# A two-layer gated-attention block: its opening, its norm factors and its layout of values

## The chip, the cores and the metric

The kernel runs on one core of a Trainium2 chip. The time is the device time of one execution in microseconds (us); the median of three executions is given. A profile of one further execution shows what each engine did. PE is TensorE, ACT is ScalarE, DVE is VectorE, POOL is GpSimd, SP is SyncE.

## The reference, cut to what matters

Two layers act on x, 512 positions of 1024 features, in f32. In each layer a root-mean-square norm stands ahead of one wide projection `w_in`, which gives queries, keys and values of three attention branches and three gates; the branches' outputs are gated, summed and projected, and a second norm and an MLP follow.

```
h = _rms_norm(x, attn_norm[l])            # x * rsqrt(mean(x*x) + 1e-6) * g
proj = h @ w_in[l]                        # a_q a_k a_v | b_ql b_kvl b_kr | c_q c_k c_v | gate
aq, ak = rope(_rms_norm(a_q)), rope(_rms_norm(a_k))   # branch A: 3 groups of 4 heads of 64
o_a = _dilated_mixture(aq, ak, a_v)
...                                       # branch B: low-rank softmax attention, 8 heads
...                                       # branch C: stick-breaking attention, 8 heads of 64
merged = gates[0]*(o_a @ wbA) + gates[1]*(o_b @ wbB) + gates[2]*(o_c @ wbC)
x = x + merged @ w_out[l]
x = x + square(relu(_rms_norm(x, mlp_norm[l]) @ w_ff1[l])) @ w_ff2[l]
```

## The kernel before

x is kept transposed, as 8 tiles of 128 features by 512 positions. Every operand of a product is split into a high and a low half (fp32r), and a product is made of three: high by high, high by low, low by high (`mm3`, L298 to L302, and the same three in `denseA`, L427 to L429). So one 128x1024 chunk of weights is loaded by SP's queue into one of two raw buffers (`wload`, L270), its high half is cast on ACT and its low half subtracted on DVE (`wsplit`, L279), both with raised priority (`Early`), and 24 products with 512 columns each use it. Chunks come in the order of `ORDER` (L36); `qk0`, the queries and keys of branch A's first group, is the first block, in 4 chunks of 2 feature tiles each; `v0`, its values and 32 shared key columns (`kr`), is the second, in 3 chunks; `g00`, a gate, is the third.

A planner orders the instructions of each engine. It takes them by priority, which is the order of the program, raised by 80 places for what is issued through `Early`, as soon as its own costs say that they are ready; on the chip each engine then runs its list in that order.

**The norm.** `norm_tile` (L382) takes one feature tile: its high half with the gain on ACT and its low half on DVE, which are the operands of the products, and its square on ACT, added up over the tiles on DVE (`nacc`; the first is copied on POOL, L392). The products use x times the gain without the norm's factor, and the factor is put on when a result leaves PSUM. `norm_end` (L396) makes that factor in two shapes. `rcol` has one value for each position on the partitions, in natural order (columns 0 to 3) and in the order of residues modulo 4 (columns 4 to 7): 16 products of `hl` by two columns of ones (L405, L406), then `rsqrt`. `rrep` has it along the free axis, the same on all partitions: two products of a matrix of ones by `hl` (L412, L413) and `rsqrt` on 128x512. `rsqrt` (L314) is Ln and Exp on ACT and three operations on DVE. In each layer `norm_end(True)` stands in the program ahead of `layer(l)`, that is ahead of `qk0`.

**The opening.** SP's queue takes x's first tile, the gains, the first chunk, x's second tile, the second chunk, the other x tiles, three tables of constants and then the further chunks, each once a raw buffer is free. ACT's first instruction loads its function table. Before the first product stand the load and the cast of the whole first chunk.

**Blocks by position.** `denseB` (L441) computes `qk0` and `v0` with the positions on the PSUM partitions, in four PSUM tiles; chunks are the outer loop, so all four tiles finish during the last chunk, and each is then evacuated on ACT with `rcol` as scale (`raw_evac`). `qk0` uses two PSUM tiles of tag `d` and two of tag `s`; `v0` uses three `d` and one `o`; `g00` takes a `d`. There are 3 `d`, 2 `s`, 2 `t` and 1 `o`. After `qk0` its queries are normed and rotated by a chain on DVE and ACT (`head_norm`, L453), transposed on PE (`to_qT`, L495), then the same for the keys (`to_kbd`, L520), which are written into a tile `kT` whose other half is zero. `kbd_open` fills those halves with four copies on DVE for each layer (L507, L508).

**Values.** A value tile holds for each head 64 high and 64 low columns (`VS`). `vs_evac` (L722) writes them with the order swapped in every second head, and so by two instructions on ACT and two on DVE for each PSUM tile, one for the even and one for the odd heads; in `v0` the `kr` columns of the same PSUM tile are read after them. The attention's last product sums the high and low rows of its output in `finish_o`, whichever stands first.

Of the kernel before, what the change touches and what calls it, by code (L numbers as in the profile page):

```python
# [223 lines left out]
class Kern:  # L224
    BUFS = dict(
        raww=2, hl=3, a4=13, x2=9, gt=3, tmp=3, ot=1, sm=8, sm8=4, sm2=4, sm8b=2, u4=16,
        raw=2, qT=2, kT=2, SN=9, PT=2, VS=1, PR=2, st=6, mx=8, PP=2, sq=2,
# [100 lines left out]

    def setup(self, es):
# [5 lines left out]
        nc.scalar.add_instruction(  # L335
            mybir.InstLoadActFuncSet(name=nc.get_next_instruction_name(), act_func_set_id=ACT_SET, ins=[], outs=[])
        )
# [3 lines left out]
        self.bcol = k([96, L, 2], "bcol")  # L341
        for j in range(KT):
# [3 lines left out]
            if j == 0:  # L346
                nc.sync.dma_start(self.gain, self.ins["gain"])
            if j in self.wl0:
                self.wload(1 + self.wl0.index(j))
# [18 lines left out]
        self.ones = k([P, P], "ones")  # L368
        nc.vector.memset(self.ones, 1.0)
        self.onesr = k([P, P], "onesr", F32R)  # L370
        nc.vector.tensor_copy(self.onesr, self.ones)
        self.zero = k([P, 1], "zero")
        nc.gpsimd.memset(self.zero, 0.0)
# [7 lines left out]
    def norm_tile(self, j, x):  # L381
# [6 lines left out]
        sq = self.t(self.cp, "tmp", [P, S])  # L388
        nc.scalar.activation(sq, x, AF.Square)
        if self.nacc is None:  # L390
            self.nacc = self.t(self.cp, "x2", [P, S])
            nc.gpsimd.tensor_copy(self.nacc, sq)  # L392
        else:
            nc.vector.tensor_tensor(self.nacc, self.nacc, sq, ALU.add)

    def norm_end(self, cols):  # L396
# [4 lines left out]
        if cols:  # L401
            pc = self.ps("o")
            for t in range(NT):
                for c, sl in ((t, slice(t * P, t * P + P)), (4 + t, slice(t, None, 4))):
                    nc.tensor.matmul(pc[:, 2 * c : 2 * c + 2], hl[:, 0, sl], self.onesr[:, :2], start=True, stop=False)  # L405
                    nc.tensor.matmul(pc[:, 2 * c : 2 * c + 2], hl[:, 1, sl], self.onesr[:, :2], start=False, stop=True)  # L406
            a = self.small()[:, :8]
            nc.vector.tensor_scalar(a, pc[:, 0:16:2], 1.0 / D, EPS, ALU.mult, ALU.add)
            self.rcol = self.kp.tile([P, 8], F32, tag="rcol", name=self.nm("rcol"))
            self.rsqrt(self.rcol, a, self.kp, "sm8", [P, 8])  # L410
# [4 lines left out]
        nc.vector.tensor_scalar(a, ps, 1.0 / D, EPS, ALU.mult, ALU.add)  # L415
        self.rrep = self.kp.tile([P, S], F32, tag="rrep", name=self.nm("rrep"))
# [15 lines left out]
    def denseB(self, names, nk, n, evac, res=False, tags="dddo"):  # L432
# [3 lines left out]
        for name, m in zip(names, nk):  # L436
            w = self.wget(name)
# [62 lines left out]
    def kbd_open(self, n):  # L500
# [221 lines left out]
    def vs_evac(self, vs, h0, col, n=4):  # L722

        def f(t, ps):
            v = vs[:, t, h0 : h0 + n].rearrange("p (a b) c -> p a (b c)", b=2)
            src = ps[:, : 64 * n].rearrange("p (a b d) -> p a b d", b=2, d=64)
            for b in range(2):
                h = v[:, :, 192 * b : 192 * b + 64]
                lo = v[:, :, 64 + 64 * b : 128 + 64 * b]
                self.split(h, lo, src[:, :, b], col[:, t : t + 1], early=True)  # L730
        return f

    def layer(self, l):
# [262 lines left out]
        def block(name, n, evac, res=False, tags="dddo"):  # L996
            nk = [3, 3, 2] if name == "v0" else [2] * 4
            self.denseB([(l, name, i) for i in range(len(nk))], nk, n, evac, res, tags)

        def d_qk(i):  # L1000
            def f():
# [9 lines left out]
                block(f"qk{i}", 512, evac, i > 0, "dddo" if i else self.qktags)  # L1011
            return f

        def d_v0():
# [296 lines left out]

    ratio = 0.8
# [5 lines left out]
    qktags = "ddss"  # L1318
# [4 lines left out]
    def run(self, es):  # L1323
# [11 lines left out]
        for l in range(L):  # L1335
            self.norm_end(True)
# [26 lines left out]
```

## Time and profile before

| what | value |
| --- | --- |
| median of 3 runs (lowest, highest) | 1842.45 us (1841.03, 1843.02) |
| the profiled execution: its time, its span | 1844.2 us, 1842.4 us |
| busy share PE, PE's weight loads, DVE, ACT, POOL | 98%, 82%, 63%, 51%, 3% |
| mean granted clock of PE | 0.997 |
| DMA, mean over the span | 101 GB/s |

Times in the rows below are in us from the span's start unless marked ns. A timeline row is: start, duration, engine, line, operation, out<-in with shapes, number of instructions, and in brackets the engine's idle time before it and what ended that. A "q" behind an engine is its sequencer. Products overlap on PE, so the distance between two starts tells their price better than their duration. L219 is the helper through which `Early` issues.

### The profile page before, as it was taken

How to read it: one execution, taken by the hardware profiler on the slowest of the kernel's cores; microseconds unless marked ns; L12 is line 12 of the kernel's file. 1: busy time of each engine (PE TensorE's matmuls, PEld its weight loads, DVE VectorE, ACT ScalarE, POOL GpSimd, SP SyncE). 2: the span in 40 equal slices, each digit the busy share in tenths (PEclk: the TensorE clock that was granted, in tenths of full speed). 3: DMA queues.
4: the chain of work that ended last, by engine and by line, in shares of the span. 5: the costliest groups of instructions: out<-in, count | busy, mean ns of one | idle time of the engine just before them, and what ended most of it. 6: DMA issues, size and time to landing. Idle time of an engine off the chain costs nothing.

```text
span 1842.4 us, 23299 instructions
## 1 busy us (share of the span) xinstructions
PE 1811.3 (98%) x8672; PEld 1518.9 (82%) x8672; DVE 1165.8 (63%) x2131; ACT 937.4 (51%) x1763; POOL 50.7 (3%) x92
## 2 busy tenths in 40 slices
PE   8999999999999999999999999999999999999999
PEld 6899888777788888888888998887777888888887
DVE  6575789969875434444565657998788753434342
ACT  5644677867744323323445456777767442323231
POOL 3000001000000000000010000000000000000000
PEclk9999999999999999999999999999999999999999
DMA  4222241232363232333322221422233533333332
GB/s 163 86 87 94 62 142 58 86 103 92 109 194 98 92 103 92 103 92 103 126 92 77 89 89 58 138 69 95 94 98 117 187 92 99 96 96 99 96 99 92
DMA packets 64705, 186.90 MB, mean 101 GB/s; under 512 B 11472, under 2 KB 11984, under 8 KB 64592
## 3 DMA queue, kind: packets, MB, share of 16 engines
q1 hardware_dynamic: 57888, 178.93, 30.3%
q0 software_dynamic: 1952, 6.29, 0.9%
q8 instruction: 69, 1.13, 0.2%
q10 hardware_dynamic: 4752, 0.18, 0.2%
q14 instruction: 44, 0.36, 0.1%
HBM read 168.55 MB, written 16.78 MB: 101 GB/s over the span
## 4 chain that ended last, share of the span: by engine, by line
PE 85%; DVE 7%; ACT 6%; issue 1%; DMA 1%; ACTq 0%; SPq 0%; DVEq 0%
PE psd L429 20%; PE psd L428 20%; PE psd L427 20%; PE psd L300 3%; PE psd L302 3%; PE psd L301 3%; PE pst L695 2%; PE pss L300 1%; DVE SN L960 1%; PE pss L951 1%; PE pss L302 1%; PE pss L301 1%; PE pso L302 1%; PE pso L300 1%; PE pso L301 1%
## 5 line engine op out<-in xcount | busy, mean ns | idle before, releaser
L219 ACT CAST hl<-raww 128x1024 fp32r<-128x1024 f32 (+1 forms) x286 | 298.4, 1044 | 651.6 <-PE psd L429 483.5
L427 PE MATMUL psd<-a,hl 128*128 128x512 f32 x1232 | 485.8, 394 | 2.2 <-ACT kr L219 2.2
L429 PE MATMUL psd<-a,hl 128*128 128x512 f32 x1232 | 485.4, 394 | 0.0
L428 PE MATMUL psd<-a,hl 128*128 128x512 f32 x1232 | 484.9, 394 | 0.0
L219 DVE TENSOR_TENSOR hl<-raww,hl 128x1024 fp32r<-128x1024 f32 (+1 forms) x286 | 346.9, 1213 | 163.5 <-ACT hl L219 163.4
L427 PEld LDWEIGHTS psd<-a,hl 128*128 128x128 f32 x1232 | 232.0, 188 | 46.5 <-ACT kr L219 2.6
L428 PEld LDWEIGHTS psd<-a,hl 128*128 128x128 f32 x1232 | 232.0, 188 | 44.9 <-issue 0.3
L429 PEld LDWEIGHTS psd<-a,hl 128*128 128x128 f32 x1232 | 232.0, 188 | 44.4
L428 PE MATMUL psd<-u,hl 128*128 128x512 f32 (+1 forms) x648 | 250.4, 386 | 0.0
L429 PE MATMUL psd<-u,hl 128*128 128x512 f32 (+1 forms) x648 | 250.4, 386 | 0.0
L427 PE MATMUL psd<-u,hl 128*128 128x512 f32 (+1 forms) x648 | 250.4, 386 | 0.0
L1300 DVE TENSOR_TENSOR x<-x,psd 128x512 f32<-128x512 f32 x63 | 43.3, 687 | 184.6 <-PE psd L429 184.6
L429 PEld LDWEIGHTS psd<-u,hl 128*128 128x128 f32 x648 | 121.7, 188 | 24.7
L427 PEld LDWEIGHTS psd<-u,hl 128*128 128x128 f32 x648 | 121.7, 188 | 24.7
L428 PEld LDWEIGHTS psd<-u,hl 128*128 128x128 f32 x648 | 121.7, 188 | 24.6
L1281 DVE SCALAR_TENSOR_TENSOR tmp<-psd,rrep 128x512 f32<-128x512 f32 x64 | 44.3, 692 | 151.5 <-PE psd L429 151.4
L300 PE MATMUL psd<-hl,a 128*128 128x512 f32 (+3 forms) x328 | 122.9, 376 | 10.4 <-ACT hl L219 7.9
L302 PE MATMUL psd<-hl,a 128*128 128x512 f32 (+3 forms) x328 | 123.5, 377 | 0.0
L301 PE MATMUL psd<-hl,a 128*128 128x512 f32 (+3 forms) x328 | 123.2, 376 | 0.0
L219 ACT ACTIVATE gt<-gt 128x512 f32<-128x512 f32 x144 | 90.3, 630 | 28.9 <-DVE gt L219 23.3
L300 PEld LDWEIGHTS psd<-hl,a 128*128 128x128 f32 x328 | 80.0, 244 | 15.4 <-ACT hl L219 7.9
L301 PEld LDWEIGHTS psd<-hl,a 128*128 128x128 f32 x328 | 80.1, 244 | 4.4 <-DVE hl L219 0.8
(249 smaller groups left out, 2455.9 us busy)
## 6 DMA issues: line engine op xcount, KB each, us to landing
raww<-w SPq DMA_DIRECT2D x278, 512.0 KB, 3.6
gpark<-gt SPq DMA_DIRECT2D x48, 256.0 KB, 2.5
gt<-gpark SPq DMA_DIRECT2D x48, 256.0 KB, 3.6
x<-xT SPq DMA_DIRECT2D x8, 256.0 KB, 6.4
x<-xT POOLq DMA_DIRECT2D x8, 256.0 KB, 4.8
park<-x POOLq DMA_DIRECT2D x8, 256.0 KB, 2.3
x<-park POOLq DMA_DIRECT2D x8, 256.0 KB, 4.6
outT<-x SPq DMA_DIRECT2D x7, 256.0 KB, 2.0
```

The costliest lines, as they stand in the source:

```text
L219: return f(*a, **k)
L300: mm(ps, ah, bh, start=start, stop=False)
L301: mm(ps, ah, bl, start=False, stop=False)
L302: mm(ps, al, bh, start=False, stop=stop)
L427: self.nc.tensor.matmul(o, w[:, 0, c : c + P], t[:, 0], start=k == 0, stop=False)
L428: self.nc.tensor.matmul(o, w[:, 0, c : c + P], t[:, 1], start=False, stop=False)
L429: self.nc.tensor.matmul(o, w[:, 1, c : c + P], t[:, 0], start=False, stop=k == last)
L695: nc.tensor.transpose(ps[:, kt * P : kt * P + P], s[:, kt * P : kt * P + P], self.ident)
L951: nc.tensor.matmul(ps[:, :m], q[:, hh, sl], k[:, i, hh, :m], start=i == 0, stop=False)
L960: nc.vector.tensor_tensor_scan(e_[:, ::-1], self.ones[:, :1].to_broadcast([P, n]), c_[:, ::-1], 0.0, ALU.mult, ALU.add)
L1281: nc.vector.scalar_tensor_tensor(t, ps, 0.0, self.rrep, ALU.max, ALU.mult)
L1300: nc.vector.tensor_tensor(x, x, ps, ALU.add)
```

## The change: what it does

- The first chunk is loaded as two transfers of half its columns, which are one feature tile each, and split by two casts and two subtractions.
- x's first tile and the gains are issued by ACT's queue, and the function table is loaded after them.
- `warm`: the matrices of ones are made first, and PE issues 8 products of them, 128x128 in plain f32, into a PSUM tile that nothing reads.
- The first square is written straight into `nacc`; POOL's copy goes.
- `norm_end(True)` is called inside `qk0`, just ahead of its fourth chunk. The 16 narrow products go; `rcol` is read off the diagonal of the 128x128 blocks of the replicated sums, by 8 multiply-and-add reductions on DVE with the identity, and its `rsqrt` is made in two halves of 4 columns.
- `kbd_open`'s four copies go from DVE to POOL.
- Values have the high columns first in every head: one instruction on ACT and one on DVE for each PSUM tile. In `v0` the `kr` columns are read first.

```diff
@@ wload, wsplit
-            self.nc.sync.dma_start(t[:, :n], src)
+            for c in self.halves(self.nload, n):
+                self.nc.sync.dma_start(t[:, c], src[:, c])
...
+    def halves(self, i, n):
+        return [slice(0, n // 2), slice(n // 2, n)] if i == 0 else [slice(0, n)]
...
-            self.hs.copy(hl[:, 0, :n], raw[:, :n])
-            self.hv.tensor_tensor(hl[:, 1, :n], raw[:, :n], hl[:, 0, :n].bitcast(F32), ALU.subtract)
+            for c in self.halves(i, n):
+                self.hs.copy(hl[:, 0, c], raw[:, c])
+                self.hv.tensor_tensor(hl[:, 1, c], raw[:, c], hl[:, 0, c].bitcast(F32), ALU.subtract)
@@ setup
+        ps = self.ps("o")
+        for i in range(self.nwarm):            # 8
+            nc.tensor.matmul(ps[:, :P], self.ones, self.ones, start=True, stop=True)
...
-            nc.sync.dma_start(xt, self.ins["xT"][j])
+            if j == 0:
+                nc.scalar.dma_start(xt, self.ins["xT"][j])
+                nc.scalar.dma_start(self.gain, self.ins["gain"])
+                nc.scalar.add_instruction(... InstLoadActFuncSet ...)
+            else:
+                nc.sync.dma_start(xt, self.ins["xT"][j])
@@ norm_tile
-        sq = self.t(self.cp, "tmp", [P, S])
+        first = self.nacc is None
+        if first:
+            self.nacc = self.t(self.cp, "x2", [P, S])
+        sq = self.nacc if first else self.t(self.cp, "tmp", [P, S])
         nc.scalar.activation(sq, x, AF.Square)
-        if self.nacc is None:
-            self.nacc = self.t(self.cp, "x2", [P, S])
-            nc.gpsimd.tensor_copy(self.nacc, sq)
-        else:
+        if not first:
             nc.vector.tensor_tensor(self.nacc, self.nacc, sq, ALU.add)
@@ norm_end
-        if cols:
-            pc = self.ps("o")
-            for t in range(NT):
-                for c, sl in ((t, slice(t * P, t * P + P)), (4 + t, slice(t, None, 4))):
-                    nc.tensor.matmul(pc[:, 2 * c : 2 * c + 2], hl[:, 0, sl], self.onesr[:, :2], start=True, stop=False)
-                    nc.tensor.matmul(pc[:, 2 * c : 2 * c + 2], hl[:, 1, sl], self.onesr[:, :2], start=False, stop=True)
...
         nc.vector.tensor_scalar(a, ps, 1.0 / D, EPS, ALU.mult, ALU.add)
+        if cols:
+            self.rcol = self.kp.tile([P, 8], F32, tag="rcol", name=self.nm("rcol"))
+            c = self.small()
+            for i in range(2):
+                for t in range(NT):
+                    sl = slice(t, None, 4) if i else slice(t * P, t * P + P)
+                    nc.vector.tensor_tensor_reduce(
+                        out=self.t(self.kp, "dg", [P, P]), in0=a[:, sl], in1=self.ident, op0=ALU.mult, op1=ALU.add,
+                        scale=1.0, scalar=0.0, accum_out=c[:, 4 * i + t : 4 * i + t + 1],
+                    )
+                self.rsqrt(self.rcol[:, 4 * i : 4 * i + 4], c[:, 4 * i : 4 * i + 4], self.kp, "sm8", [P, 4])
@@ denseB(..., last=None)
+            if last is not None and name is names[-1]:
+                last()
             w = self.wget(name)
@@ kbd_open
-            nc.vector.tensor_copy(k[0:64, :, 1, :], z[0:64].to_broadcast([64, 2, S]))
-            nc.vector.tensor_copy(k[64:128, :, 0, :], z[64:128].to_broadcast([64, 2, S]))
+            nc.gpsimd.tensor_copy(k[0:64, :, 1, :], z[0:64].to_broadcast([64, 2, S]))
+            nc.gpsimd.tensor_copy(k[64:128, :, 0, :], z[64:128].to_broadcast([64, 2, S]))
@@ vs_evac
-            v = vs[:, t, h0 : h0 + n].rearrange("p (a b) c -> p a (b c)", b=2)
-            src = ps[:, : 64 * n].rearrange("p (a b d) -> p a b d", b=2, d=64)
-            for b in range(2):
-                h = v[:, :, 192 * b : 192 * b + 64]
-                lo = v[:, :, 64 + 64 * b : 128 + 64 * b]
-                self.split(h, lo, src[:, :, b], col[:, t : t + 1], early=True)
+            v = vs[:, t, h0 : h0 + n]
+            src = ps[:, : 64 * n].rearrange("p (h d) -> p h d", d=64)
+            self.split(v[:, :, 0:64], v[:, :, 64:128], src, col[:, t : t + 1], early=True)
@@ d_qk, d_v0, run
+                    block("qk0", 512, evac, False, "ddss", lambda: self.norm_end(True))
...
             def evac(t, ps):
+                self.hs.activation(kr[:, t], ps[:, 256:288], AF.Copy, scale=self.rcol[:, t : t + 1])
                 ev(t, ps)
-                self.hs.activation(kr[:, t], ps[:, 256:288], AF.Copy, scale=self.rcol[:, t : t + 1])
...
-            self.norm_end(True)
             self.layer(l)
```

## Rows read from the trace of the kernel before

**Rows 1.** The page's first part: busy us, share of span, instructions of each engine.
```profile
PE 1811.3 (98%) x8672; PEld 1518.9 (82%) x8672; DVE 1165.8 (63%) x2131; ACT 937.4 (51%) x1763; POOL 50.7 (3%) x92
```
**Rows 2.** Waits of PE, whole span: who, for whom, us in total, times, longest.
```profile
PE psd L300 <- ACT hl L219: 7.9, 1, 7.9
...
PE psd L427 <- ACT kr L219: 2.2, 2, 1.1
...
PE pst L520 <- DVE raw L475: 2.1, 4, 0.9
```
**Rows 3.** Stretches after sparse PE work: length, busy by engine, clock, DMA share, GB/s.
```profile
26.20:30.10 3.90, 3.90 (x12) 3.04 (x12) 2.31 (x6) 1.95 (x5) 0.15 (x1) 0.56 0.18 68
...
933.20:938.20 5.00, 5.00 (x16) 3.97 (x16) 3.70 (x8) 1.68 (x4) 0.00 (x0) 0.66 0.44 141
965.10:973.00 7.90, 5.92 (x26) 4.58 (x25) 6.25 (x16) 4.83 (x12) 0.00 (x0) 0.78 0.37 133
```
**Rows 4.** The chain of waits in the opening: start us, us, what.
```profile
1.65 5.14 DMA raww<-w
```
**Rows 5.** Timeline of ACT in the opening.
```profile
3.54 0.63 ACT L389 ACTIVATE tmp<-x 128x512 f32<-128x512 f32 x1 [1.52 <-DMA x<-xT]
```
**Rows 6.** Timeline of PE, first layer's opening.
```profile
7.92 1.22 PE L300 MATMUL psd<-hl,a 128*128 128x512 f32 x2 [7.92 <-ACT hl L219]
...
11.05 0.63 PE L302 MATMUL psd<-hl,a 128*128 128x512 f32 x1
...
11.48 0.63 PE L301 MATMUL psd<-hl,a 128*128 128x512 f32 x1
...
23.59 0.17 PE L406 MATMUL pso<-onesr,a 128*128 128x2 f32 x1
...
26.14 0.47 PE L301 MATMUL psd<-hl,a 128*128 128x512 f32 x1
...
38.07 0.29 PE L300 MATMUL psd<-hl,a 128*128 128x288 f32 x1
```
**Rows 7.** Timeline of DVE and POOL, first layer's opening.
```profile
15.12 1.14 POOL L360 CAST masksb<-masks 128x1152 bf16<-128x1152 f32 x1 [0.41 <-DMA masks<-con]
15.18 1.63 DVE L312 SCALAR_TENSOR_TENSOR a<-x,gain,a 128x512 fp32r<-128x512 f32 x1
...
19.70 1.59 DVE L394 TENSOR_TENSOR x<-x,tmp 128x512 f32<-128x512 f32 x2
...
21.20 1.27 DVE L219 TENSOR_TENSOR hl<-raww,hl 128x1024 fp32r<-128x1024 f32 x1
```
**Rows 8.** Timeline of PE, second layer's opening.
```profile
924.37 0.39 PE L300 MATMUL psd<-hl,a 128*128 128x512 f32 x1
924.59 0.39 PE L301 MATMUL psd<-hl,a 128*128 128x512 f32 x1
...
930.47 0.27 PE L406 MATMUL pso<-onesr,a 128*128 128x2 f32 x1
...
933.13 0.48 PE L301 MATMUL psd<-hl,a 128*128 128x512 f32 x1
...
951.42 0.29 PE L300 MATMUL psd<-hl,a 128*128 128x288 f32 x1
```
**Rows 9.** Groups by shape, whole span: count, busy us, mean ns, idle before.
```profile
L530 DVE CUSTOM_DVE_ANT_0 SN<-pss,masksb 128x128 f32<-128x128 f32 x24 | 6.5, 283 | 2.3 <-PE pss L302 2.3
...
L507 DVE CAST kT<-zero 64x1024 fp32r<-64x1024 f32 x4 | 2.8, 703 | 0.0
...
L219 DVE SCALAR_TENSOR_TENSOR VS<-psd,rcol,VS 128x128 fp32r<-128x128 f32 x12 | 4.0, 345 | 0.1
```
**Rows 10.** Groups by shape, ACT and POOL, whole span.
```profile
L219 ACT ACTIVATE VS<-psd,rcol 128x256 fp32r<-128x256 f32 x12 | 5.3, 472 | 3.9 <-PE psd L302 2.4 <-DVE VS L219 1.5
...
L219 ACT ACTIVATE VS<-psd,rcol 128x128 fp32r<-128x128 f32 x12 | 4.1, 363 | 1.4 <-PE psd L302 1.4
...
L687 POOL CAST PP<-zero 128x256 fp32r<-128x256 f32 x8 | 3.0, 402 | 144.9 <-PE pso L713 128.9 <-PE pso L678 16.0
```

More of the change, by code (lines that the diff above doesn't have):

```diff
@@ L226 @@
         raww=2, hl=3, a4=13, x2=9, gt=3, tmp=3, ot=1, sm=8, sm8=4, sm2=4, sm8b=2, u4=16,
-        raw=2, qT=2, kT=2, SN=9, PT=2, VS=1, PR=2, st=6, mx=8, PP=2, sq=2,
+        dg=1, raw=2, qT=2, kT=2, SN=9, PT=2, VS=1, PR=2, st=6, mx=8, PP=2, sq=2,
         qT_B=4, SN_B=4, SN_C=3, SR_C=2,
@@ L326, in small, with warm @@
         return self.t(self.cp, "sm", shape or [P, 32])
+    def warm(self, k):
+        nc = self.nc
+        self.zero = k([P, 1], "zero")
+        nc.gpsimd.memset(self.zero, 0.0)
+        self.ones = k([P, P], "ones")
+        nc.vector.memset(self.ones, 1.0)
+        self.onesr = k([P, P], "onesr", F32R)
+        nc.vector.tensor_copy(self.onesr, self.ones)
+        ps = self.ps("o")
+        for i in range(self.nwarm):
+            nc.tensor.matmul(ps[:, :P], self.ones, self.ones, start=True, stop=True)
     def setup(self, es):
@@ L341, in setup @@
         self.bcol = k([96, L, 2], "bcol")
+        self.warm(k)
         for j in range(KT):
             xt = self.t(self.cp, "x2", [P, S])
-            nc.sync.dma_start(xt, self.ins["xT"][j])
+            if j == 0:
+                nc.scalar.dma_start(xt, self.ins["xT"][j])
+                nc.scalar.dma_start(self.gain, self.ins["gain"])
+                nc.scalar.add_instruction(
+                    mybir.InstLoadActFuncSet(name=nc.get_next_instruction_name(), act_func_set_id=ACT_SET, ins=[], outs=[])
+                )
+            else:
+                nc.sync.dma_start(xt, self.ins["xT"][j])
             self.x.append(xt)
-            if j == 0:
-                nc.sync.dma_start(self.gain, self.ins["gain"])
             if j in self.wl0:
@@ L367, in setup @@
         ctmp.close()
[L368 to L373, printed above, removed]
     def norm_begin(self, goff, l):
@@ L400, in norm_end @@
         self.split(hl[:, 0], hl[:, 1], self.nacc)
-        if cols:
-            pc = self.ps("o")
-            for t in range(NT):
-                for c, sl in ((t, slice(t * P, t * P + P)), (4 + t, slice(t, None, 4))):
-                    nc.tensor.matmul(pc[:, 2 * c : 2 * c + 2], hl[:, 0, sl], self.onesr[:, :2], start=True, stop=False)
-                    nc.tensor.matmul(pc[:, 2 * c : 2 * c + 2], hl[:, 1, sl], self.onesr[:, :2], start=False, stop=True)
[L407 to L410, printed above, removed]
         ps = self.ps("o")
@@ L415, in norm_end @@
         nc.vector.tensor_scalar(a, ps, 1.0 / D, EPS, ALU.mult, ALU.add)
+        if cols:
[7 more added lines that the diff above has]
+                        scale=1.0, scalar=0.0, accum_out=c[:, 4 * i + t : 4 * i + t + 1],
+                    )
+                self.rsqrt(self.rcol[:, 4 * i : 4 * i + 4], c[:, 4 * i : 4 * i + 4], self.kp, "sm8", [P, 4])
         self.rrep = self.kp.tile([P, S], F32, tag="rrep", name=self.nm("rrep"))
@@ L430, in denseA, with denseB @@
         return ps
-    def denseB(self, names, nk, n, evac, res=False, tags="dddo"):
+    def denseB(self, names, nk, n, evac, res=False, tags="dddo", last=None):
         pss = [self.ps(tags[t]) for t in range(NT)]
@@ L993, in raws, with block @@
             return t[:, : 4 * nh * d].rearrange("p (t h d) -> p t h d", t=4, h=nh)
-        def block(name, n, evac, res=False, tags="dddo"):
+        def block(name, n, evac, res=False, tags="dddo", last=None):
             nk = [3, 3, 2] if name == "v0" else [2] * 4
-            self.denseB([(l, name, i) for i in range(len(nk))], nk, n, evac, res, tags)
+            self.denseB([(l, name, i) for i in range(len(nk))], nk, n, evac, res, tags, last)
         def d_qk(i):
@@ L1009, in evac @@
                     ek(t, ps[:, 256:])
-                block(f"qk{i}", 512, evac, i > 0, "dddo" if i else self.qktags)
+                if i:
+                    block(f"qk{i}", 512, evac, True)
+                else:
+                    block("qk0", 512, evac, False, "ddss", lambda: self.norm_end(True))
             return f
@@ L1310, in xsrc @@
         return self.ins["xT"][j] if l == 0 else self.park[j]
+    nwarm = 8
     ratio = 0.8
```

4 lines of the change are left out of this document (removed).

## The prediction

> **What bounds the kernel now.** I read the page's busy shares first, then PE's waits, then the two openings by stretches and timelines. PE is busy 98% of the span [rows 1]; no other engine comes near. So time is gained only where PE does work that need not be done, runs at half clock, or stands still. The waits [rows 2] show where it stands: 7.9 us once, for the first cast high half of weights; 2.2 us in two waits of 1.1 before a gate (L427), whose PSUM tile is held until ACT has read `kr`; 2.1 us before the transposes of keys (L520). The granted clock is lower in three stretches only [rows 3], each behind sparse work of PE: one in the first layer's opening (mean 0.56) and two in the second's (0.66, 0.78). At half clock two products start 0.43 us apart (starts 11.05 and 11.48 [rows 6]), at full clock 0.22 to 0.23 (starts 924.37 and 924.59 [rows 8]); I use 0.23. `qk0` has 4 chunks x 24 = 96 products, so it needs 22.1 us. It takes 38.07 - 7.92 = 30.15 us in the first layer [rows 6] and 951.42 - 924.37 = 27.05 us in the second [rows 8]. What the change can reach lies mostly in these 8.1 and 5.0 us, in the 7.9 us ahead and in the waits behind.
>
> **Second layer's opening** (the simpler one). The narrow products go from 930.47 to 933.13 [rows 8]: 2.7 us. The slow clock behind them, mean 0.66 over 5.0 us [rows 3], lost (1 - 0.66) x 5.0 = 1.7 us of clock; it should go with the narrow products, as nothing else in that stretch is sparse. The two replicated products stay (2 x 0.23). 27.05 - 22.1 - 0.46 = 4.5 us, which is 2.7 + 1.7 and 0.1 of small gaps. PE has nothing to wait for there: feature tiles and chunks come at the MLP's pace. The replicated products now come behind the third chunk in priority, so perhaps only 72 x 0.23 = 16.6 us after 924.4, at 941.0; then one DVE pass over 512 columns (0.69, as L394 has nearly the same size: 1.59 for two [rows 7]), four diagonal reads, and a short `rsqrt`. One diagonal read has the size of the 128x128 masked reduction, 0.28 us [rows 9]; a 512-column add, 0.8, is the other bound, so 8 cost 2.3 (at most 6.4) us per layer on DVE. The four copies taken off DVE cost 4 x 0.70 = 2.8 [rows 9], so DVE comes out even. The first four factors are there at about 941.0 + 0.7 + 1.1 + 1.3 (`rsqrt` on few columns, five short steps, my estimate from 0.2 to 0.3 each as the narrowest rows show) = 944; the first tile of `qk0` ends at about 924.4 + 80 x 0.23 = 942.8. Its evacuation waits 1.3 us, but `v0` can start in the third `d` tile and needs the second only at 948. Cost: 0.1. Value: 4.4 us.
>
> **First layer's opening.** The first product needs x's first tile, there at 3.54 [rows 5], and the chunk: issued at 1.65, under way 5.14, landed at 6.79 [rows 4], cast, product at 7.92. Afterwards half the chunk is first on SP's queue and x's first tile first on ACT's. It lands not before 3.5, when one transfer of that size alone lands now, and not after 5.2, half way to 6.79. Behind it ACT has up to three operations of 0.63 [rows 5] before PE can start: 4.1 to 7.1. I take 5.9, for two transfers side by side and three operations: 2.0 us earlier. Two queue moves come with it: the table load now stands behind two issues on ACT, hidden as x lands only at 3.5; and every transfer behind on SP moves forward by one place, with the third chunk still behind all x tiles and the constants.
> The narrow products take 23.59 to 26.14, 2.55 us, and the slow clock behind them (1 - 0.56) x 3.9 = 1.7. The first 11 products, at half clock, lose about 11 x 0.2 = 2.2. If all of this counted the gain would be 2.0 + 8.1 - 0.46 = 9.6. It does not, because of DVE: it works without a pause until the sum of squares ends at 21.29, and subtracts the third chunk's low half from 21.20 to 22.47 [rows 7]. PE now arrives there at about the right moment. Afterwards it would have finished two chunks at 5.9 + 48 x 0.23 = 17 (19.4 if the first 11 are slow), and DVE is ahead by only the first chunk's subtraction, 1.2 us, which moves into DVE's idle time before 7.9. So the third chunk is whole at about 21.2; the 32 of its and the fourth's products that use no low half of weights can begin when its high half is cast, some 1.5 us before. I let the third and fourth chunk start at 20.0: 20.0 + 48 x 0.23 + 0.46 = 31.5 and, for a slow stretch behind the idle time with chance one half, 0.8 more: 32.3. Gain 38.07 - 32.3 = 5.8 us; between 3.8 (start at 21.2, slow clock) and 7.6 (start at 19.0, none).
> **The unread products** therefore count nothing in my sum: whether PE's first 11 products are slow is lost again in the wait for the third chunk. They end before PE has other work: 8 x 0.06 (a quarter of 512 columns) to 8 x 0.43 us from about 1 on, so at 4.5 at most. POOL's copy of the first square, too, was off DVE's path: nothing.
>
> **POOL's four fills.** POOL needs 0.40 us for 128x256 [rows 10]; 1024 columns cost between 0.70 (DVE's) and 1.6, so 2.8 to 6.4 us a layer. They come after the rotary tables, where POOL idles, and the first half-zero tile is needed 15 us or more later. Do they hinder DVE? At 15.12 POOL's cast takes 1.14, and a DVE operation that begins at 15.18 takes 1.63, twice the 0.8 of its neighbours [rows 7]: it ended only after POOL's. Each fill can so delay one of DVE's operations by up to its own length, and in the first layer they fall among the diagonal reads. The factors are needed when `qk0` ends; 0.4 us is what I let this cost, the bounds are 0 and 6.4.
> The Trainium skill has a rule for this ("SBUF — State Buffer", section "Who interferes with whom"): VectorE and GpSimd share one pair of ports, and a VectorE instruction with two inputs in SBUF and a GpSimd instruction that reads SBUF shut each other out for the whole instruction. The row at 15.18 agrees. By it the diagonal reads, which have both inputs in SBUF, are the wrong kind of work to put beside fills that read SBUF; it leads to the last rival below.
>
> **Values.** Two ACT operations of 0.363 become one of 0.472, on DVE two of 0.345 one of about 0.47 [rows 9, 10]: 0.25 and 0.22 us less per tile, on engines with room. What matters is the order: the second ACT operation waited for DVE's first, and `kr` for both. With `kr` first and one pair, the PSUM tile that L427 waits for is free earlier, and of 2 x 1.1 us [rows 2] I count 1.2 for both layers (0 to 2.2; the next limit is the keys' transposes, 0.9 earlier in the row). The slow clock there in the second layer, (1 - 0.78) x 7.9 = 1.7 us [rows 3], stands behind that wait; with half the chance that it goes, 0.8. The first layer has the same wait without the slow clock.
>
> **Sum.** 4.4 + 5.8 - 0.4 + 1.2 + 0.8 = 11.8 us from the profiled execution's 1844.2, whose span is 1842.4 with 1.8 around it: 1832.4. It stood 1.75 above the median of the runs shown, so for the median 1842.45 - 11.8 = 1830.6. From there to the end PE is the bound and nothing outside paces it (DMA moves 101 GB/s on average), so what the openings gain is kept. One thing can't be priced from rows: the planner's lists change, and PE's other 19 us of idle time (1842.4 - 1811.3 - 12.2 [rows 1, 2]), mostly short waits in the attention phases, may come out 2 us either way.
>
> **The rivals.**
> *PE waits for the third chunk or the factors as long as it gained.* For it: DVE without a pause to 22.47 and POOL's hold on it [rows 7]. Against: DVE has 1.2 us less ahead of that point. The first layer keeps 2.55 from the narrow products alone, the waits behind `v0` stay: 4.4 + 2.55 = 7, 1835.5. Chance 0.19.
> *Everything counts.* DVE's list puts the third chunk before the last sums, PE keeps full clock: 4.5 + 9.6 + 2.2 + 1.7 = 18 at best, 15.5 with part of the waits: 1827. Against it: the same [rows 7]. Chance 0.12.
> *The change hardly does what it says.* The planner puts the replicated products late, evacuation and the chain behind it follow, and the waits behind `v0` grow by what `qk0` saved in each layer; only the earlier start (2.0) and some clock remain: within 3.7 of before, 1840.5. Chance 0.08.
> *Slower: fills against diagonal reads.* If all four fills (6.4 us) and two chunk subtractions (2.5) get in ahead of the factors, these are 8.9 us late. The slack is about 4 (`v0` takes its second `d` tile 1.2 us after `qk0`, the factors are due 3 before its end). Then PE stands 4.9 us in each layer at `v0`'s second tile, a slow clock behind that costs 1.7, and the head norms' chain is late by as much again at the keys' transposes: 2 x (4.9 + 1.7 + 2) = 17 against a gain of 11.8: 1848. It is slower than before from a delay of the factors by some 7 us on. Against it: in the second layer the fills end long before the replicated products. Chance 0.04.
>
> **How the numbers follow.** The forecast has 0.57, with a range of its own from 1828 to 1834. For 8 in 10 I cut the upper rivals at 1838.5 and the lower at 1825. A measurement of this kernel tells 0.2% (3.7 us) from no change: faster 0.57 + 0.19 + 0.12 and little less for spread, 0.87; within it 0.09; slower 0.04.
>
> **What would show it.** First product at 5.5 to 6.5; `qk0` ends near 32 in the first layer, with an idle PE of 1 to 4 us before its third chunk; in the second it takes 22.5 to 23.5 us and the clock stays up. No product of two columns. PE's wait at L427 for `kr` below 0.6 each. Eight reductions of 0.3 us on DVE, fills of 1.2 to 1.6 on POOL. I am wrong if PE waits at `v0`'s second tile, if a slow stretch remains in the second layer's `qk0`, or if the attention phases' waits change by more than 2 us.

## The result, and the profile after

The changed kernel takes 1831.3 us (median of 4 runs, 1830.5 to 1832.1); the kernel before took 1841.7 beside it (4 runs, 1840.7 to 1843.0). The ratio is 0.9943, 95% interval 0.9926 to 0.9960: 10.4 us faster. The forecast was 1830.6.

The profiled execution took 1830.46 us with a span of 1828.7. It is 13.8 us shorter than the one profiled before, 3.4 more than the medians differ. The busy line of the page answers to [rows 1]: 16 narrow products a layer are gone from PE and 8 unread ones have come (each counts as two records), and DVE's total hardly moves.

```profile
PE 1803.8 (99%) x8656; PEld 1515.2 (83%) x8656; DVE 1161.4 (64%) x2136; ACT 931.0 (51%) x1744; POOL 56.9 (3%) x96
```

PE's waits of the changed kernel, whole span (who, for whom, us in total, times, longest), beside [rows 2]:

```profile
PE psd L306 <- ACT raw L219: 2.0, 1, 2.0
PE psd L306 <- ACT a L317: 2.0, 1, 2.0
...
PE pso L418 <- ACT a L314: 0.9, 1, 0.9
...
PE psd L444 <- DVE VS L219: 0.3, 1, 0.3
PE pst L539 <- DVE raw L494: 0.3, 2, 0.2
```

The waits of 1.1 for `kr` and of 0.9 for the keys are gone, and the 7.9 ahead of the first product are now 2.0 behind the unread products. The first line is new: it is the wait at `v0`'s second tile that the prediction named as a sign of error. PE's timeline in the changed kernel shows the places (start us, us, instruction, idle before it), first and second layer, against [rows 6, 8]:

```profile
6.55 0.50 PE L306 MATMUL psd<-hl,a 128*128 128x512 f32 x1 [1.97 <-ACT a L317]
...
21.15 0.49 PE L418 MATMUL pso<-a,onesr 128*128 128x512 f32 x1 [0.87 <-ACT a L314]
...
32.02 0.29 PE L306 MATMUL psd<-hl,a 128*128 128x288 f32 x1
...
35.42 0.40 PE L306 MATMUL psd<-hl,a 128*128 128x288 f32 x1 [2.04 <-ACT raw L219]
...
918.55 0.39 PE L306 MATMUL psd<-hl,a 128*128 128x512 f32 x1
...
940.76 0.29 PE L306 MATMUL psd<-hl,a 128*128 128x288 f32 x1
```

`qk0` ends at 32.02 instead of 38.07 in the first layer, and takes 22.21 instead of 27.05 us in the second. With the start of the last product of each `v0`, and of DVE's multiplication for the last gate of each layer, from the timelines of both kernels, the profiles divide so (us):

| stretch | before | after | gained in sum |
| --- | --- | --- | --- |
| start to `qk0`'s end, layer 1 | 38.07 | 32.02 | 6.05 |
| `v0`, layer 1 (the new wait) | 13.60 | 15.82 | 3.83 |
| behind `v0` to the last gate, layer 1 | 480.33 | 478.37 | 5.79 |
| output and MLP, layer 1 | 392.37 | 392.34 | 5.82 |
| `qk0`, layer 2 | 27.05 | 22.21 | 10.66 |
| `v0`, layer 2 | 13.60 | 13.53 | 10.73 |
| behind `v0`, layer 2 | 481.16 | 478.19 | 13.70 |
| output and MLP, layer 2 | 396.27 | 396.20 | 13.77 |

Two windows of the changed kernel (length, busy by engine, granted clock, DMA share, GB/s) answer to [rows 3]. The second layer's `qk0` keeps the higher clock (1.00). The one stretch at 0.50 stands in the first layer's opening, behind the idle time of 1.97 us between the unread products and the first real one.

```profile
7.60:11.00 3.40, 3.40 (x10) 2.66 (x9) 2.83 (x5) 3.40 (x7) 0.00 (x0) 0.50 1.05 385
...
918.50:940.70 22.20, 22.20 (x99) 18.39 (x99) 11.46 (x27) 7.38 (x11) 10.98 (x18) 1.00 0.31 91
```

Clock explains most of the 3.4 us. The profiled execution of before lies 2.5 us above its median, the one of the changed kernel 0.8 below its own. The former had three stretches with half clock in them [rows 3], each worth 1.7 us, and the mean clock of other executions of the same kernel says that they had other numbers of them: in one set of 21 the span was 1836.6 to 1837.4 at a mean clock of 1.000 (five executions), 1840.5 and 1840.6 at 0.998, 1843.4 and 1843.9 at 0.996. The median, with a span near 1840, so holds fewer of them than the profile.

### The profile page after: what moved, and what is told of

Same layout as the page of the kernel before. It is cut to its first block, busy times and chain, and to the rows that moved or that the text cites. A ratio compares the mean times of both kernels' runs of the same rounds, so it can differ in the third digit from the quotient of the medians.

```text
span 1828.7 us, 23259 instructions
## 1 busy us (share of the span) xinstructions
PE 1803.8 (99%) x8656; PEld 1515.2 (83%) x8656; DVE 1161.4 (64%) x2136; ACT 931.0 (51%) x1744; POOL 56.9 (3%) x96
## 4 chain that ended last, share of the span: by engine, by line
PE 84%; DVE 7%; ACT 5%; issue 2%; DMA 1%; ACTq 0%; DVEq 0%
PE psd L446 21%; PE psd L445 21%; PE psd L444 21%; PE psd L306 3%; PE psd L308 3%; PE psd L307 3%; PE pst L714 2%; DVE SN L976 1%; PE pss L967 1%; PE pss L306 1%; DVE hl L219 1%; PE pss L307 1%; PE pss L308 1%; PE pst L514 1%; PE pso L695 1%
## 5 line engine op out<-in xcount | busy, mean ns | idle before, releaser
L219 ACT CAST hl<-raww 128x1024 fp32r<-128x1024 f32 (+3 forms) x287 | 298.6, 1041 | 655.5 <-PE psd L446 479.4
L219 DVE TENSOR_TENSOR hl<-raww,hl 128x1024 fp32r<-128x1024 f32 (+3 forms) x287 | 347.8, 1212 | 159.5 <-ACT hl L219 159.1
```

The lines of the kernel that those rows point to most:

```text
L219: return f(*a, **k)
```

## The experiments

Medians stand beside 1831.3 for the changed kernel; each ratio is to the kernel before in the same set. Unless said otherwise each kernel is the changed one with the edit shown.

**The changed kernel again**, unedited, shows the spread.

> The changed kernel once more, to have its time beside the others on one chip. 1831.3 us +- 1, ratio to before 0.994; PE waits 2.0 us at v0's second PSUM tile in the first layer.

1831.31 us (1831.2 to 1832.7), 0.9942 [0.9929, 0.9955]. In this profile PE's products are 0.43 us apart until 12.4, where in the first profile they were 0.23 apart at the beginning and slow from 7.6 to 11.0; `qk0` takes 25.46 against 25.47 us. What the opening's slow products cost is lost again in the wait for the sums of squares, as forecast. (The granted clock reads 1.00 over those products, 6.62 to 12.33, though their distance is that of half clock; only the distance shows it.) The wait at `v0`'s second tile is 2.46 us here, and behind it stands this execution's one stretch of lower granted clock:

```profile
35.90:39.90 4.00, 4.00 (x18) 4.00 (x19) 1.22 (x3) 3.92 (x11) 0.00 (x0) 0.57 0.00 0
```

It loses (1 - 0.57) x 4.0 = 1.7 us, and `v0` takes 17.77 instead of 15.82. So the wait can cost nearly twice its length.

**POOL's fills.** The wait at `v0`'s second tile is for ACT's evacuation, which is for `rcol`. The timeline of POOL and DVE in the changed kernel, where the first layer's factors are made:

```profile
25.14 1.03 POOL L526 CAST kT<-zero 64x1024 fp32r<-64x1024 f32 x1
...
28.14 1.04 POOL L526 CAST kT<-zero 64x1024 fp32r<-64x1024 f32 x1
...
28.57 1.52 DVE L219 TENSOR_TENSOR hl<-raww,hl 128x864 fp32r<-128x864 f32 x1 [0.34 <-ACT hl L219]
...
29.22 1.77 POOL L527 CAST kT<-zero 64x1024 fp32r<-64x1024 f32 x1
...
30.01 1.12 DVE L428 CUSTOM_DVE_ANT_0 dg<-tmp,ident 128x128 f32<-128x128 f32 x1
...
34.28 0.16 DVE L329 SCALAR_TENSOR_TENSOR rcol<-sm,sm 128x4 f32<-128x4 f32 x1
```

The chunk's subtraction beside the fill that begins at 28.14 takes 1.52 us, and the diagonal read beside the next one takes 1.12 and ends just behind it. In the next two runs the same kinds take 1.06 and 0.29. The fills on DVE again:

```diff
-            nc.gpsimd.tensor_copy(k[0:64, :, 1, :], z[0:64].to_broadcast([64, 2, S]))
+            nc.vector.tensor_copy(k[0:64, :, 1, :], z[0:64].to_broadcast([64, 2, S]))
...
```

> Changed kernel with the zero fills back on DVE. The 2.0 us wait of PE at v0's second tile (factors ready at 34.4) has two possible causes. PORT: POOL's fills shut DVE out; the lengthened DVE operations add up to 1.6 us (1.52 for 1.05, 1.12 and 0.47 for 0.29). Then without fills on POOL DVE's operations have their usual lengths, but 4 x 0.70 us of fills stand in DVE's own list: factors at 33.6 to 35.6, wait 1.2 to 3.2. ORDER: the second replicated product is queued behind the third chunk (26.4 where its input is there at 22.3), the short chain follows 4 us late: wait 2 or more. Time by PORT 1831 to 1832, by ORDER 1832 to 1833.

1829.98 us (1829.8 to 1833.0), 0.9936 [0.9924, 0.9949]. The first four reads take 0.28 to 0.29, PE's wait at `v0`'s second tile is 0.8. The fills still on POOL, but written as constants:

```diff
-            nc.gpsimd.tensor_copy(k[0:64, :, 1, :], z[0:64].to_broadcast([64, 2, S]))
+            nc.gpsimd.memset(k[0:64, :, 1, :].bitcast(F32), 0.0)
...
```

> Changed kernel with the fills still on POOL, but as memset, which reads nothing. PORT (and the rule that only a POOL instruction that reads SBUF shuts out DVE's two-input operations): diagonal reads back at 0.29, chunk subtraction at 1.05, factors at 32.8, wait at v0's second tile 0.4, time 1.6 us under the changed kernel (1829.7). ORDER: factors at most 0.5 earlier, wait 1.5 or more, time unchanged.

1830.31 us (1829.6 to 1830.7), 0.9934 [0.9921, 0.9947]: all five executions are shorter than all five of the changed kernel run again above. The groups by shape of this kernel (busy us, mean ns of one, idle before):

```profile
L527 POOL MEMSET kT<- 64x1024 f32 x4 | 3.8, 950 | 0.2
```

Its timeline of POOL, DVE and PE at the same place:

```profile
27.43 0.95 POOL L526 MEMSET kT<- 64x1024 f32 x1
...
28.10 0.29 DVE L428 CUSTOM_DVE_ANT_0 dg<-tmp,ident 128x128 f32<-128x128 f32 x1
...
28.41 0.95 POOL L527 MEMSET kT<- 64x1024 f32 x1
...
28.85 1.06 DVE L219 TENSOR_TENSOR hl<-raww,hl 128x864 fp32r<-128x864 f32 x1 [0.45 <-ACT hl L219]
...
33.27 0.16 DVE L329 SCALAR_TENSOR_TENSOR rcol<-sm,sm 128x4 f32<-128x4 f32 x1
...
34.41 0.40 PE L306 MATMUL psd<-hl,a 128*128 128x288 f32 x1 [0.75 <-ACT raw L219]
```

The read at 28.10 lies almost wholly inside a fill and the subtraction at 28.85 begins inside the next; both take their usual time. So it is not POOL's work that hinders DVE but what POOL reads: the casts from the zero column do, the constants don't. (One later read takes 0.48, at 29.83, beside another of POOL's casts from that column.) The Trainium skill says this in "SBUF — State Buffer", section "Who interferes with whom": a GpSimd instruction that only writes does not enter the contest for the shared ports. The run with constants agrees (1.06 and 0.29 us beside a fill, against 1.52 and 1.12 beside a cast). The wait that remains, 0.75, has another cause.

**The factors one chunk earlier**, to test whether the order of the program sets that wait:

```diff
-            if last is not None and name is names[-1]:
+            if last is not None and name is names[-2]:
```

> Changed kernel with norm_end called ahead of qk0's third chunk, not its fourth. ORDER: the replicated products run at about 22.4, the factors are there by 28, PE does not wait at v0's second tile; v0 ends 2 us earlier in the first layer (45.8), the second layer's qk0 stays at 22.2; time 1829.3. PORT: the fills at 25 to 31 still lengthen DVE's operations and 1 us or more of the wait stays, time 1830.5.

1833.52 us (1831.9 to 1835.0), 0.9951 [0.9937, 0.9964]: 2.2 us slower than the changed kernel by the medians, with two of six executions among its times. Timeline of DVE and PE in it:

```profile
26.01 1.47 DVE L327 SCALAR_TENSOR_TENSOR tmp<-tmp 128x512 f32<-128x512 f32 x1
27.40 1.15 DVE L428 CUSTOM_DVE_ANT_0 dg<-tmp,ident 128x128 f32<-128x128 f32 x1
...
28.47 1.92 DVE L219 TENSOR_TENSOR hl<-raww,hl 128x864 fp32r<-128x864 f32 x1
...
42.72 0.66 PE L514 MATMUL pst<-ident,raw 128*128 128x128 f32 x4 [3.12 <-DVE raw L494]
```

The reads are earlier but now meet the casts (25.70 to 31.30); `rcol` is written at 33.02 all the same, the queries come late, and PE waits 3.12 us for them. Both expectations were too low. Order alone is no remedy while the casts stand there. Both edits together:

```diff
-            nc.gpsimd.tensor_copy(k[0:64, :, 1, :], z[0:64].to_broadcast([64, 2, S]))
+            nc.gpsimd.memset(k[0:64, :, 1, :].bitcast(F32), 0.0)
...
-            if last is not None and name is names[-1]:
+            if last is not None and name is names[-2]:
```

> Changed kernel with memset fills and norm_end ahead of the third chunk together. In the run with norm_end early alone the fills lengthened DVE's operations between 26.0 and 32.7 by 3.6 us. If PORT and ORDER both held, the factors now come at 33.0 - 3.6 = 29.4, ahead of qk0's end (32.2): no wait at v0's second tile, none at the queries' transposes, 0.7 us under the memset kernel: 1829.5. If the early call itself is what hurts (PE's list has the transposes too early), the 3.1 us wait at the transposes stays and the time is 1832 or more.

1829.52 us (1828.7 to 1830.4), 0.9933 [0.9921, 0.9946]; `rcol` is written at 29.80 and PE no longer waits at `v0`'s second tile. A subtraction from 26.98 on, beside fills all the time (26.77 to 28.73), takes 1.06. This has the lowest median, 1.8 us below the changed kernel; by the ratios it can't be told from the two runs without the casts (0.9933 against 0.9934 and 0.9936).

**The diagonal undone**: the 16 products of two columns again, at the changed kernel's place inside `qk0`.

```diff
-        if cols:
-            self.rcol = ...
...
+        if cols:
+            pc = self.ps("o")
+            for t in range(NT):
+                for c, sl in ((t, slice(t * P, t * P + P)), (4 + t, slice(t, None, 4))):
+                    nc.tensor.matmul(pc[:, 2 * c : 2 * c + 2], hl[:, 0, sl], self.onesr[:, :2], start=True, stop=False)
...
```

> Changed kernel with the 16 narrow products of two columns back for the factors, called at the same place in qk0. The forecast gave the diagonal 2.7 us of PE in each layer and 1.7 of slow clock behind: second layer's qk0 22.2 -> 25 (26.7 with a slow stretch), first layer's 25.5 -> 26 to 28; time 4 to 8 us over the changed kernel, 1835 to 1839. Rival: PE had room in the first layer, and the short chain after narrow products gives earlier factors and takes the 2.0 us wait away: 2.5 over, 1834.

1834.22 us (1832.4 to 1835.6), 0.9958 [0.9944, 0.9972]: 2.9 us slower. In its profile the first and the last narrow product of the second layer are, in the timeline of PE,

```profile
936.54 0.17 PE L421 MATMUL pso<-onesr,a 128*128 128x2 f32 x1
...
938.97 0.37 PE L422 MATMUL pso<-onesr,a 128*128 128x2 f32 x1
```

and the window over most of that `qk0` (granted clock third from the end) is

```profile
925.00:947.00 22.00, 22.00 (x96) 18.47 (x95) 6.20 (x11) 6.97 (x13) 6.54 (x7) 0.92 0.23 75
```

In that execution `qk0` costs 4.5 us more in the first and 4.4 in the second layer: the products and a slow stretch ((1 - 0.92) x 22.0 = 1.8 us) in each. But PE doesn't wait at `v0`'s second tile (2.2 back), and 0.9 comes back behind `v0` in each layer. The factors from the diagonal are the later ones: with the narrow products all of `rcol` is written 3.8 and 5.4 us ahead of `qk0`'s end; in the changed kernel its first half is written 2.4 us behind it in the first layer and 0.1 behind in the second. The net is 5.2 us in this profile and 2.9 in the medians.

**The values undone**: two layouts and `kr` last.

```diff
-                self.hs.activation(kr[:, t], ps[:, 256:288], AF.Copy, scale=self.rcol[:, t : t + 1])
                 ev(t, ps)
+                self.hs.activation(kr[:, t], ps[:, 256:288], AF.Copy, scale=self.rcol[:, t : t + 1])
...
-            v = vs[:, t, h0 : h0 + n]
-            src = ps[:, : 64 * n].rearrange("p (h d) -> p h d", d=64)
-            self.split(v[:, :, 0:64], v[:, :, 64:128], src, col[:, t : t + 1], early=True)
+            ...
+            for b in range(2):
+                h = v[:, :, 192 * b : 192 * b + 64]
+                lo = v[:, :, 64 + 64 * b : 128 + 64 * b]
+                self.split(h, lo, src[:, :, b], col[:, t : t + 1], early=True)
```

> Changed kernel with the old layout of values, two operations per engine and tile, kr last. The forecast gave it 1.2 us of waits and 0.8 of clock: 1.2 to 4 us slower (1832.5 to 1835), PE waits about 1 us at the gate behind v0 in each layer. Rival: the gain behind v0 came from the shorter chain of factors and the fills, and the layout is worth under 0.5 us.

1840.83 us (1838.6 to 1844.5), 0.9998 [0.9989, 1.0007]. This was the surprise: all other edits together gain nothing that can be measured. The openings are as fast as in the changed kernel (`qk0` ends at 32.05, and takes 22.22 us in the second layer). The loss stands behind `v0`: 5.9 us in the first, 3.1 in the second layer. PE's waits in this kernel (total, times, longest):

```profile
PE psd L444 <- ACT kr L219: 6.8, 2, 3.4
```

The first of the two in PE's timeline:

```profile
51.71 0.80 PE L444 MATMUL psd<-a,hl 128*128 128x512 f32 x1 [3.42 <-ACT kr L219]
```

And the window behind it, at half clock:

```profile
51.70:57.70 6.00, 5.99 (x14) 4.74 (x15) 2.88 (x8) 0.86 (x3) 0.00 (x0) 0.50 0.25 87
```

Part of the 9.5 us is clock: the eleven executions have a middle mean clock of 0.997, those of the changed kernel 0.999, and 0.002 of 1838 are 3.7 us. The rest is mostly waits. Before, the waits for `kr` were 1.1 [rows 2]. Why are they 3.4 here? The keys' last operation ahead of their transposes ends in the kernel before at 52.80, 0.8 us behind `v0`'s last product (timelines of PE and DVE):

```profile
51.67 0.29 PE L302 MATMUL pso<-hl,a 128*128 128x288 f32 x1
...
52.38 0.42 DVE L475 TENSOR_TENSOR raw<-tmp,tmp 128x256 f32<-128x256 f32 x1
```

and in the changed kernel at 53.90, 5.8 us behind it:

```profile
47.84 0.29 PE L308 MATMUL pso<-hl,a 128*128 128x288 f32 x1
48.26 0.50 PE L444 MATMUL psd<-a,hl 128*128 128x512 f32 x1
...
53.48 0.42 DVE L494 TENSOR_TENSOR raw<-tmp,tmp 128x256 f32<-128x256 f32 x1
...
53.96 0.66 PE L539 MATMUL pst<-ident,raw 128*128 128x128 f32 x4
```

In the second layer the distances are the same, 0.8 and 5.8 us. So on PE the gate's 24 products stand ahead of the keys' transposes, 48.26 to 53.96 in the changed kernel's timeline, with no idle time. In exchange nothing stands between `v0` and the gate any more while the gate's PSUM tile is being read.

Why are the keys later? That `rcol` is there only at or behind `qk0`'s end is not enough. In the run with narrow products it is written 3.8 us ahead of `qk0`'s end, and the keys still come 4.3 us behind `v0`'s last product (50.39 to 50.68), behind the gate (timelines of DVE and PE in that run):

```profile
32.83 0.17 DVE L329 SCALAR_TENSOR_TENSOR rcol<-sm,sm 128x8 f32<-128x8 f32 x1
...
36.75 0.29 PE L306 MATMUL psd<-hl,a 128*128 128x288 f32 x1
...
50.53 0.40 PE L443 MATMUL psd<-a,hl 128*128 128x512 f32 x1
...
54.60 0.41 DVE L493 TENSOR_TENSOR raw<-tmp,tmp 128x256 f32<-128x256 f32 x1
...
55.34 0.60 PE L538 MATMUL pst<-ident,raw 128*128 128x128 f32 x4
```

With `norm_end` called a chunk earlier the keys end only 0.6 us (casts) and 1.0 us (constants) behind, in the first of these although `rcol`'s first half is written only at 33.17, behind `qk0`'s end at 32.20. So the place of the call sets the order. Three runs test what the values' edit is worth in either order.

The kernel before with the values' edit alone:

```diff
+                self.hs.activation(kr[:, t], ps[:, 256:288], AF.Copy, scale=self.rcol[:, t : t + 1])
                 ev(t, ps)
-                self.hs.activation(kr[:, t], ps[:, 256:288], AF.Copy, scale=self.rcol[:, t : t + 1])
...
-            for b in range(2):
...
+            self.split(v[:, :, 0:64], v[:, :, 64:128], src, col[:, t : t + 1], early=True)
```

> The kernel before with one edit: the new layout of values and kr read first. Three theories. TERM (the forecast): this edit takes 1.2 us off the waits behind v0 and 0.8 off a slow clock, so about 2 us: 1839.8 where the kernel before has 1841.8; PE's waits for kr (2.2) and for the keys' raw tile (2.1) fall below 2.5 together. LAYOUT (the edit is worth what undoing it cost in the changed kernel, wherever it stands): 9.5 us, 1832. LATE KEYS (the cost of undoing it came from the changed order: there the gate's products stand ahead of the keys' transposes, so PE stands still until the values' chain has read the PSUM tile): here the transposes still come early, so 1.5 to 3 us, 1839 to 1840.5.

1838.75 us (1836.1 to 1841.0), 0.9984 [0.9976, 0.9993]: 3.5 us by the medians, 2.9 by the ratio. PE waits 0.69 in each layer, at the gate's first product, instead of 0.89 and 1.08 in two places:

```profile
52.52 0.50 PE L427 MATMUL psd<-a,hl 128*128 128x512 f32 x1 [0.69 <-DVE VS L219]
```

The edit alone is not worth 9.5; that figure belongs to the changed kernel. That it needs the later call among that kernel's edits is argued from the order above: the old values with the call a chunk earlier and constant fills were not run.

In the changed kernel, `kr` last alone:

```diff
-                self.hs.activation(kr[:, t], ps[:, 256:288], AF.Copy, scale=self.rcol[:, t : t + 1])
                 ev(t, ps)
+                self.hs.activation(kr[:, t], ps[:, 256:288], AF.Copy, scale=self.rcol[:, t : t + 1])
```

> The changed kernel with kr read after the values again, the new layout kept. KR ORDER (the 3.4 us waits of the run with both undone come from kr's place): PE waits over 2.5 us at the gate in each layer, 1838 or more. PAIRS (they come from the two alternations of ACT and DVE for each tile in the old layout): with one pair kr waits for one DVE operation more, at most 1 us in each layer, 1831.3 to 1833.5.

1836.52 us (1834.1 to 1838.1), 0.9967 [0.9957, 0.9976]. And the old layout alone:

```diff
-            self.split(v[:, :, 0:64], v[:, :, 64:128], src, col[:, t : t + 1], early=True)
+            for b in range(2):
...
+                self.split(h, lo, src[:, :, b], col[:, t : t + 1], early=True)
```

> The changed kernel with the old layout of values again, kr read first. PAIRS: the PSUM tile is held until the second DVE operation for it has read it, at 51.33 where kr ended the holding at 51.65 with both undone; so PE waits about 3 us at the gate in each layer, with a slow clock behind it in some executions: 1838 to 1841. KR ORDER: the wait is below 1 us and the time 1831 to 1833.

1835.17 us (1834.1 to 1835.6), 0.9968 [0.9955, 0.9980]. The gate's first product in the first layer, timeline of PE, with `kr` last

```profile
52.08 0.50 PE L444 MATMUL psd<-a,hl 128*128 128x512 f32 x1 [1.89 <-ACT kr L219]
```

and with the old layout

```profile
50.29 0.50 PE L444 MATMUL psd<-a,hl 128*128 128x512 f32 x1 [1.66 <-DVE VS L219]
```

Neither theory of mine holds alone. I had put nearly all of the 3.4 on the two pairs of the old layout; they make 1.66, the place of `kr` makes 1.89, and the changed kernel has 0.0 and 0.3. The two halves add up to the whole, in waits (3.6 against 3.4) and nearly in time (5.2 and 3.9 us against 9.5).

In the version with constant fills and the earlier call the keys' last operation ends at 47.73, 1.0 us behind `v0`'s last product, much as in the kernel before, and their transposes stand behind the gate's first products only, at 48.02. The gate then waits 0.7 for the values.

**No unread products**: 0 instead of 8.

```diff
-    nwarm = 8
+    nwarm = 0
```

> Changed kernel without the 8 unread products. The forecast counts them at nothing: first products at half clock until 10 to 13 us, PE reaches the third chunk 1 to 2 us later, where it waits anyway; qk0 ends at 32.0 +- 0.6, time unchanged within 0.7. Rival: the clock they bring is worth its 2.2 us: qk0 ends at 34, time 1833.5.

1830.85 us (1830.4 to 1831.1), 0.9941 [0.9928, 0.9953]: no loss. The first product comes at 6.46, products are 0.43 apart until 9.6 and 0.23 from 10.0, and `qk0` ends at 32.18, 0.16 behind the changed kernel.

**The first chunk whole.**

```diff
-        return [slice(0, n // 2), slice(n // 2, n)] if i == 0 else [slice(0, n)]
+        return [slice(0, n)]
```

> The changed kernel with the first chunk in one transfer, one cast and one subtraction. COUNTED: the first product comes at 7.3 to 7.6 instead of 6.55, as the whole chunk lands at about 5.5 and its cast takes 1.04 behind or ahead of the cast of x, and all of it reaches the end: 0.8 to 1.1 us, 1832.2. ABSORBED (the third chunk and the sums of squares set the pace before qk0's end, as the forecast let the unread products' gain vanish there): qk0's end in the first layer moves by less than 0.3 us, 1831.4.

1832.08 us (1831.9 to 1834.3), 0.9956 [0.9942, 0.9969]. The timelines of ACT and PE in it:

```profile
6.33 0.72 ACT L317 ACTIVATE a<-x,gain 128x512 fp32r<-128x512 f32 x1 [3.37 <-DMA gain<-gain]
6.95 1.03 ACT L219 CAST hl<-raww 128x1024 fp32r<-128x1024 f32 x1
...
8.04 1.22 PE L306 MATMUL psd<-hl,a 128*128 128x512 f32 x2 [3.19 <-ACT hl L219]
```

The first product is 1.49 us later and `qk0` ends 1.22 later, so most of what the halves give counts. The medians differ by 0.8, less than their spread can tell.

The moves of x's first tile, the gains and the table load, and the first square without POOL's copy, were not undone by themselves; no run prices them.

## Why the prediction was right, step by step

*Second layer's opening*, 4.4 forecast: 4.84 in the profile, no slow clock, no wait. The mechanism was right. Its part in the medians is smaller, since 1.7 of it was a slow stretch that not every execution has, and since the later call would have cost something behind `v0` without the values' edit.

*First layer's opening*, 5.8: 6.05. The first product comes at 6.55, not 5.9: both halves had landed by 5.49, but the cast of x's first tile waited for the gains. Timeline of ACT in the changed kernel:

```profile
4.42 0.62 ACT L219 CAST hl<-raww 128x512 fp32r<-128x512 f32 x1 [1.48 <-DMA raww<-w]
5.77 0.72 ACT L317 ACTIVATE a<-x,gain 128x512 fp32r<-128x512 f32 x1 [0.73 <-DMA gain<-gain]
```

I had looked at the chunk and at x and not at the third operand, whose transfer had been moved with x. An earlier first product would have gained little: PE stands again for 0.87 before 21.15, for the sums of squares, and does not stop from there to 32.02. A later one does cost, 1.22 for 1.49 in the run with the whole chunk. I had 20.0 to 21.2 for that point and 31.5 to 32.3 for the end. I took the products at 11.05 and 11.48 [rows 6] for half clock; their distance says so, and is the same where the granted clock reads 0.50 (27.09 and 27.52), but the clock recorded over 9.20 to 12.60 is 1.00.

*Unread products*, 0: 0, by the run without them.

*POOL's fills*, 0.4: a term that was mis-sized. The two runs without the casts are 1.3 and 1.0 us faster, and the mechanism was the one from [rows 7], told as the slower rival. That rival's size was wrong too: the delay stays in the first layer, it is 2.0 to 2.5 us at `v0`'s second tile and not 4.9, and 0.7 of it is the order, which goes when the factors stand a chunk earlier and the fills are constants. The slow clock of 1.7 that the rival put behind this wait came in one of the two profiles.

The estimate of the factors' time in the second layer, 944, counts from an opening at 924.4, 19.6 us on. Measured from the opening at 918.55 it is 22.3 (timeline of DVE):

```profile
940.66 0.16 DVE L329 SCALAR_TENSOR_TENSOR rcol<-sm,sm 128x4 f32<-128x4 f32 x1
```

So it was 2.7 us too early. The replicated products were not late (16.3 against 16.6); the sum left out that DVE's list would put a chunk's subtraction (1.05) and the three steps for `rrep` (0.69 each) ahead of the reads and among them. PE has no wait there, so the cost of 0.1 held.

*Values*, 1.2 + 0.8 = 2.0: 1.96 in the first and 2.97 in the second layer of the profile, together 4.9, of which 1.7 is the slow stretch. By itself, in the kernel before, the edit gives 2.9 to 3.5 us. The step that failed is treating it as a term of its own. I costed the late evacuation of `qk0` at 0.1, since PE has `v0` to do, and that is so; but behind it, with the later call, the keys come 5 us later against `v0`, the gate moves ahead of them, and what PE waits behind `v0` rises from 2.0 to 3.4 in each layer. With the values' edit it is 0.0 and 0.3 here, and up to 0.8 in the other profiles with this layout and order. The third rival, waits behind `v0` that grow by what `qk0` saved, is what the changed kernel would have been without that edit: 1840.8 against 1840.5 there.

*Sum.* The profile gained 13.8, the forecast 11.8, the medians 10.4. The forecast took three slow stretches from one execution as if each run had them; at a mean clock of 1.000 the spans of the kernel before were 1836.6 to 1837.4 in one set, and the two such executions of the changed kernel had 1829.3 and 1829.4. By these, 7 to 8 us are work and waits, and the rest of the 10.4 is clock. So the time came out 0.7 us from the forecast with two errors that partly cancel: the clock counted too high, the waits behind `v0` too low. That the middle was met so closely is luck.

*Named signs.* The first product came at 6.55 (5.5 to 6.5 forecast), PE's idle time at the third chunk was 0.87 (1 to 4), the second layer's `qk0` took 22.21 (22.5 to 23.5), POOL's fills 1.03 to 1.85 (1.2 to 1.6): all just outside. No slow stretch in the second layer's `qk0`: right. `kr`'s wait below 0.6: right. A wait at `v0`'s second tile: it came, and with it the 1.0 to 1.3 us above. The attention's other waits moved by less than 1 us (the longest group, for `SN`, from 5.3 to 6.1).

## What to carry to other kernels

Parts of a change that touch the same PSUM tiles are not a sum: here the openings alone gave nothing, the values alone 3, both 10, and the timelines put that on the later call of `norm_end`, with which a gate moved ahead of the transposes that used to cover its tile's readers. When work is moved to POOL, ask what it reads: a fill that only writes left DVE alone, one that copies a zero stretched DVE's two-input operations beside it (0.29 to 1.12, 1.06 to 1.52 us). And count slow-clock stretches over several executions, not from one profile.

## What was not expected of the hardware

- A fill of 64x1024 takes POOL 0.95 us as a constant, beside DVE's work or not; as a cast it takes 1.03 to 1.85 and stretches the DVE operation beside it (0.28 to 1.12, 1.06 to 1.92 us, the latter with the earlier call).
- Stretches at half clock come and go between executions of one kernel; the kernel before spreads from 1838 to 1847 us with them, at mean clocks from 1.000 to 0.995. They stood behind the narrow products and behind waits of PE of 1.1 to 3.4 us. Unread products that are followed by 2 us of idle time did not keep the clock up: in one execution it fell at 7.6, in another products were 0.43 us apart until 12.4, without them until 9.6. The granted clock showed only the first of these.
